# A decoder layer whose instruction order is planned by a list scheduler: new durations and ranks, q split before it is stored, gates kept as sums, small loads issued second

## The chip, the core and the metric

The kernel runs on one core of one Trainium2 chip. The core has five engines, each with an instruction queue of its own that is worked off in order: TensorE (PE, matmuls, with its weight loads shown apart as PEld), VectorE (DVE), ScalarE (ACT), GpSimd (POOL) and SyncE (SP, which here only issues DMA transfers). DMAs are also issued from the queues of ACT and POOL. The metric is the device time of one execution in microseconds; the median of several executions is compared.

## The reference

One layer (DEPTH = 1) on 1024 tokens of 1024 channels, in float32:

```python
h = rms_norm(x, g_mix_norm[l])
z = h @ w_in[l]
q, kc, vc, ks_, vs_, kw_, vw_, gl, hc, cg, bg = jnp.split(z, offs, axis=-1)
q = rms_norm(q.reshape(B, T, N_ATTN_HEADS, HEAD_DIM), g_q[l])
k_cmp = rms_norm(compress(kc...), g_k[l, 0])
v_cmp = compress(vc...)
k_slc = rms_norm(ks_.reshape(kv_shape), g_k[l, 1])
k_win = rms_norm(kw_.reshape(kv_shape), g_k[l, 2])
gates = jax.nn.sigmoid(gl).reshape(B, T, N_ATTN_HEADS, N_BRANCH)
attn_out = nsa_attention(q, k_cmp, v_cmp, k_slc, vs_, k_win, vw_, gates)
conv_out = short_conv_mixer(hc, cg, bg, conv_w[l])
mixed = jnp.concatenate([rms_norm(attn_out, ...), rms_norm(conv_out, ...)], axis=-1)
x = x + mixed @ w_o[l]
h = rms_norm(x, g_ffn_norm[l])
x = x + jnp.square(jax.nn.relu(h @ w_up[l])) @ w_down[l]
```

There are 8 query heads of 64 channels in 2 groups that share keys and values. Each head has three softmax branches with a distance penalty: over 63 compressed blocks, over selected blocks (with 1024 tokens all 16 blocks are chosen), and over a window of 512 tokens. Each branch's output is multiplied by its gate, sigmoid(gl) = 1 / (1 + exp(-gl)), and the three are added. `compress` is a small MLP with a tanh-approximated GELU over blocks of 32 tokens. The feed-forward part is 1024 to 4096 to 1024 with a squared ReLU.

## The kernel before

**Numbers and tiles.** Tokens are worked in eight blocks of 128 (`tb`). Each float32 factor of a matmul is split in a high part, rounded to the matmul's input type, and a low part, the rest; a product is three matmuls, high by high, high by low and low by high (`mm3`). A split is one ACT copy for the high part and one subtraction on DVE or POOL for the low one (`split_psum`, `w_piece`, `split`).

**Stages, in the order of the source.**
1. The token blocks are normalised and transposed (`norm_in`); five small loads fill the tile `rows` (norm gains, convolution weights, position terms), which PE transposes into `cols`; the weight splits scale by columns of `cols`.
2. The input projection by tokens (`z_tokens`): keys and values (stored to `kv_d` or split), then the window part with the gates, then q. Between its matmuls the steps of the compression MLP run (`compress_steps`: tiles `ch`, `araw`, `ah`, `al`, `hp`, `hx`, `hT`, `cps`).
3. The rest of the projection by channels (`z_chan`, tile `zc`) and the convolution.
4. The convolution's half of the output projection (`wc`), key transposes, and attention: per block of queries and group, `queries` loads and transposes q (`qx`, `tpq`, `Qg`, `Qz`), `scores` makes scores, row minima and exponentials, and `weigh` transposes the probabilities, multiplies by the values (`ot`, `ops`, `ot_s`, `osb`) and weighs with `rr`; `finish` adds attention's half of the output projection.
5. The up projection in 16 pairs (`pair`), as products of sums of quadrants (a seven-product scheme; operands B11, T2, ... and sums S1 to S4), whose results are stored in `u_d`; then the down projection in 8 rounds, which loads them again (`ur`, split as `uu`), splits the weight sums (`we`) and adds each result to `y`.

**Who sets the order.** Nothing of this runs in source order. Every operation is first recorded as a node of a `Plan`, with the nodes that it has to wait for; `cost` gives each its duration by engine, operation and columns; `schedule` then simulates the engines and orders the nodes, and `issue` emits them in that order. So the order inside each engine's queue is fixed beforehand; on the chip an instruction that waits holds everything behind it. All recorded operations carry one line number, L261, in the profile; they are told apart by their tiles. In `schedule` a node's rank (`prio`) is the longest path from it to the end, along its successors and the reuse of tile buffers; an engine that is free takes the ready node of highest rank. Before, up to four matmuls in a row on the same output tile are one node:

```python
GROUP = 4
```

An engine is busy for `busy`, and the result counts as there after `late`. All DMAs share one modelled line of 0.36 MB per us plus 1.75 us. Engines don't disturb each other in the model, only that DVE's two-input operations on 256 columns or more outside PSUM count 1.45 times; a power on POOL counts 0.5 us whatever its size.

**q before.** In the q loop of `trunk_layer`, a block's result is copied out of PSUM by ACT (`z`, two buffers), squared and reduced; POOL makes the reciprocal root by a power (`rsqrt`, with `rs_t` and `qri`); then eight multiplications on DVE, one for each head, write the normalised row twice, side by side, into `qn` (one buffer), and ACT issues the store to `q_d`. Later `queries` loads both copies, transposes them, ACT rounds both to the high part (`Qg`), and DVE subtracts in the half of partitions that shall hold the low part.

**Gates before.** `gates` holds 1 / (1 + exp(-gl)) for all tokens; `scores` takes the reciprocal of the three sums of exponentials (`sm`) and multiplies by the gates, one small DVE operation for each branch, into `rr`.

Of the kernel before, what the change touches and what calls it, by code (L numbers as in the profile page):

```python
# [18 lines left out]
P = 128  # L19
# [4 lines left out]
H = 8  # L24
# [109 lines left out]
class Node:  # L134
    def __init__(self, k, engine):
        self.k, self.engine, self.do, self.preds, self.succ = k, engine, [], set(), []
        self.busy = self.late = self.bytes = 0.0
        self.base, self.bases = None, []
# [11 lines left out]
class Plan:  # L150
# [82 lines left out]
    def op(self, name, engine, method, a, kw):  # L233
        views = [("" if i else "out", v) for i, v in enumerate(a)] + list(kw.items())
        views = [(k, v) for k, v in views if isinstance(v, View)]
        preds, touched = set(), []
        for k, v in views:
# [5 lines left out]
            for n, ow, o0, o1, om in v.base.seen:  # L243
                if (w or ow) and r0 < o1 and o0 < r1 and m & om:
                    preds.add(n.k)
        out = views[0][1] if views else None
        last = self.last_pe if name == "PE" else None
# [7 lines left out]
        node.preds |= preds  # L255
        if name == "PE":
# [12 lines left out]
        busy, late, size = self.cost(name, method, a, kw, views)  # L269
        node.late = node.busy + late  # L270
        node.busy += busy
        node.bytes += size
# [4 lines left out]
    GROUP = 4  # L277

    def cost(self, name, method, a, kw, views):
        n = max([v.cols() for _, v in views], default=1)  # L280
        psum = any(v.base.pool.psum for k, v in views if k not in ("out", "accum_out"))
        if method == "dma_start":
            nb = 4 * max(int(np.prod(v.shadow.shape)) for _, v in views)
            return (.75 if name == "POOL" else .33), 0.0, nb
        if name == "PE":
# [6 lines left out]
            return c, c + .17, 0  # L292
        if name == "ACT":
            c = .06 + n * .00093 if n >= 600 else max(.085 + n * .00079 if n > 100 else .17 + n * .0008, .17)
            acc = kw.get("accum_out") is not None
            return c + .1 * acc, c + (.1 if acc else .11), 0
        if name == "DVE":
            if method == "tensor_tensor_reduce":
                return .135 + n * .00125, .19 + n * .0013, 0
            if method == "tensor_tensor":  # L300
                c = (.06 + n * .00106) * (1.45 if not psum and n >= 256 else 1.0)
            elif method == "scalar_tensor_tensor":
                c = .06 + n * (.00112 if n > 600 else .00122)
            elif method == "tensor_scalar":
                c = .06 + n * .00085
            else:
                c = .06 + n * .00106
            return max(c, .08), c + .08, 0
        if method == "tensor_tensor":
            if kw.get("op") == ALU.pow:  # L310
                return .5, .56, 0
            c = .18 + n * .00215
            return c, c + .03, 0
        c = .15 + n * .0009 if method == "tensor_copy" else .12 + n * .0008 if method == "memset" else .2 + n * .002
# [3 lines left out]
    def schedule(self, weight=lambda n: 0.0, rings=True):  # L318
        nodes = self.nodes
        slots, held, left_of = {}, {}, {}  # L320
        for b in self.bases:
            slots[id(b.ring)] = [0.0] * b.ring[0]
            held[id(b.ring)] = []
            left_of[b] = [len(b.nodes), 0.0]
# [27 lines left out]
        for n in nodes:  # L352
            n.prio += weight(n)
# [4 lines left out]
        line, order, end = 0.0, [], 0.0  # L358
# [9 lines left out]
        while True:  # L368
            while stack:
                n = stack.pop()  # L370
                if n.engine is None:
                    if n.base is not None:
# [4 lines left out]
                        n.ready = max(n.ready, heapq.heappop(slots[ring]))  # L377
# [20 lines left out]
            n = nodes[heapq.heappop(ready[e])[1]]  # L398
            n.start = t
            free[e] = t + n.busy  # L400
            done = t + n.late
            if n.bytes:
                line = max(t + .4, line) + n.bytes / .36e6
                done = line + 1.75
            end = max(end, done)
            order.append(n)
            for b in n.bases:
                rest = left_of[b]
                rest[0] -= 1
                rest[1] = max(rest[1], done)  # L410
                if not rest[0]:
                    heapq.heappush(slots[id(b.ring)], rest[1])
                    stack.extend(held[id(b.ring)])
                    held[id(b.ring)] = []
            if n.bytes:
                settle(n, done)
            else:
                for s in n.succ:
                    s.left -= 1
                    s.ready = max(s.ready, t + n.busy if s.engine == n.engine else done + .05 * (s.engine is not None))  # L420
                    if not s.left:
                        stack.append(s)
# [15 lines left out]
def trunk_layer(ctx, tc, x, g_mix_norm, w_in, g_q, g_k, pe_cmp, w_cmp1, b_cmp1, w_cmp2, b_cmp2,  # L438
# [50 lines left out]
    gates = cst.tile([P, NT, 3 * H], F32, name="gates")  # L489
# [961 lines left out]
```

## Time and profile before

| | us |
|---|---|
| median of 3 runs | 1324.02 |
| lowest, highest | 1319.44, 1326.87 |
| the profiled execution | 1318.85 |
| its span, first to last instruction | 1317.1 |

The mean granted clock of TensorE in that execution was 0.991. How to read the rows that follow: an instruction row has its start, its duration, the engine, what it writes and reads, and, in brackets, how long the engine stood idle before it and what released it. A matmul's duration holds its passage through the array, so matmuls overlap; the rate is read from their starts. PE's busy time is the union of such stretches, so that a busy PE can still run slowly. ACTq and SPq mark DMA issues from the queues of ACT and SP. A duration from issue to landing is that of the whole transfer.

### The profile page before, as it was taken

The numbers are of one execution on the slowest core, as the hardware profiler recorded it, in microseconds if no ns is written. First come the engines' busy times: TensorE is split into PE (matmuls) and PEld (weight loads), VectorE is DVE, ScalarE is ACT, GpSimd is POOL, SyncE is SP. The second block draws the span as 40 slices with busy tenths as digits, with TensorE's granted clock in tenths as the row PEclk, the third lists the DMA queues.
The fourth block names the chain that finished last, engine by engine and source line by source line (L and its number), as shares of the span: only waits on it lengthen the run. The fifth ranks groups of instructions, "written<-read, shape, count | busy, mean of one in ns | idle before, by whom it ended". The sixth has DMA issues, their size and how long they took to land. (4 is left out here: it accounts for less than half of the span.)

```text
span 1317.1 us, 18392 instructions
## 1 busy us (share of the span) xinstructions
PE 1248.7 (95%) x6170; PEld 1031.2 (78%) x6170; DVE 909.9 (69%) x1869; ACT 674.1 (51%) x1498; POOL 672.9 (51%) x583
## 2 busy tenths in 40 slices
PE   6999899999889999999899999999999899999998
PEld 5897688888678888888777877777777687777787
DVE  6466864434698899998874655555657777887875
ACT  6343542211588988887956454445333343434441
POOL 2243311221133333112766877777879977788761
PEclk9999899999999999999899999999999999999999
DMA  6253431212310000000414435345339445443423
GB/s 223 77 137 112 127 90 51 73 38 80 112 65 33 33 33 33 25 15 4 128 64 168 135 137 168 123 149 168 137 134 395 142 160 168 152 130 122 149 64 128
DMA packets 91575, 147.66 MB, mean 112 GB/s; under 512 B 10901, under 2 KB 45801, under 8 KB 91481
## 3 DMA queue, kind: packets, MB, share of 16 engines
q1 hardware_dynamic: 87256, 134.51, 31.1%
q10 hardware_dynamic: 3456, 9.44, 1.9%
q0 software_dynamic: 768, 2.56, 0.7%
q8 instruction: 48, 0.79, 0.2%
q14 instruction: 47, 0.38, 0.1%
HBM read 102.43 MB, written 44.04 MB: 111 GB/s over the span
## 5 line engine op out<-in xcount | busy, mean ns | idle before, releaser
L261 PE MATMUL X<-we,uu 128*128 128x512 f32 x768 | 186.4, 393 | 13.3 <-DVE y L261 7.3
L261 PEld LDWEIGHTS X<-we,uu 128*128 128x128 f32 x768 | 144.0, 189 | 49.1 <-issue 7.0
L261 PE MATMUL Z<-we,uu 128*128 128x512 f32 x576 | 139.0, 392 | 2.7 <-DVE y L261 2.7
L261 PEld LDWEIGHTS Z<-we,uu 128*128 128x128 f32 x576 | 109.1, 190 | 25.9 <-ACT uu L261 3.1
L261 POOL TENSOR_TENSOR d<-d 128x512 f32<-128x512 f32 x64 | 96.8, 1523 | 21.7 <-DVE d L261 20.6
L261 ACT ACTIVATE we<-wd 128x512 fp32r<-128x512 f32 x64 | 40.5, 632 | 124.6 <-PE X L261 83.6
L261 DVE TENSOR_TENSOR y<-X,y 128x512 f32<-128x512 f32 x128 | 79.4, 681 | 33.8 <-PE X L261 33.7
L261 DVE TENSOR_TENSOR pl<-tp,ph 128x512 fp32r<-128x512 f32 (+1 forms) x148 | 95.2, 655 | 9.1 <-ACT ph L261 8.6
L261 ACT ACTIVATE pt<-pt,nm 128x640 f32<-128x640 f32 (+7 forms) x128 | 93.8, 735 | 11.5 <-DVE nm L261 11.2
L261 POOL TENSOR_TENSOR uu<-ur,uu 128x512 fp32r<-128x512 f32 x56 | 80.0, 1432 | 32.7 <-ACT uu L261 32.7
L261 ACT ACTIVATE ph<-tp 128x512 fp32r<-128x512 f32 (+1 forms) x148 | 82.5, 573 | 20.1 <-PE tp L261 18.2
L261 PE MATMUL tp<-ident,pt 128*128 128x128 f32 x528 | 88.7, 275 | 3.4 <-ACT pt L261 1.7
L261 DVE SCALAR_TENSOR_TENSOR w_lo<-w_raw,cols,w_hi 128x128 fp32r<-128x128 f32 (+3 forms) x128 | 56.0, 491 | 43.3 <-ACT w_hi L261 43.2
L261 PEld LDWEIGHTS tp<-ident,pt 128*128 128x128 f32 x528 | 65.5, 140 | 21.2 <-ACT pt L261 4.3
L261 ACT ACTIVATE w_hi<-w_raw,cols 128x128 fp32r<-128x128 f32 (+3 forms) x128 | 53.1, 486 | 54.5 <-PE zc L261 27.0
L261 DVE TENSOR_TENSOR we<-s,we 128x512 fp32r<-128x512 f32 x42 | 41.6, 990 | 56.4 <-ACT we L261 51.9
L261 DVE TENSOR_TENSOR uu<-ur,uu 128x512 fp32r<-128x512 f32 x56 | 66.7, 1195 | 17.8 <-ACT uu L261 17.8
L261 ACT ACTIVATE wu<-wu,cols 128x256 f32<-128x256 f32 x128 | 55.8, 509 | 37.2 <-DMA wu<-in_w_up_dram 37.2
L261 DVE TENSOR_TENSOR we<-wu,we 128x512 fp32r<-128x512 f32 x38 | 50.5, 1341 | 34.1 <-ACT we L261 34.1
L261 PE MATMUL zc<-hTl,w_hi 128*128 128x512 f32 x192 | 71.8, 389 | 0.0
L261 DVE TENSOR_TENSOR y<-Z,y 128x512 f32<-128x512 f32 x96 | 59.5, 682 | 17.6 <-PE Z L261 17.6
L261 POOL TENSOR_TENSOR osb<-osb,ot_s 128x256 f32<-128x256 f32 x64 | 48.4, 756 | 45.2 <-DVE ot_s L261 39.1
(1262 smaller groups left out, 3562.6 us busy)
## 6 DMA issues: line engine op xcount, KB each, us to landing
u_d<-d SPq DMA_DIRECT2D x112, 256.0 KB, 2.1
ur<-u_d SPq DMA_DIRECT2D x112, 256.0 KB, 3.0
wu<-in_w_up_dram SPq DMA_DIRECT2D x16, 1024.0 KB, 6.0
wd<-in_w_down_dram SPq DMA_DIRECT2D x16, 1024.0 KB, 6.8
w_raw<-in_w_in_dram SPq DMA_DIRECT2D x20, 512.0 KB, 3.7
xt<-in_x_dram SPq DMA_DIRECT2D x10, 512.0 KB, 5.6
w_raw<-in_w_cmp_dram SPq DMA_DIRECT2D x8, 512.0 KB, 4.0
q_d<-qn ACTq DMA_DIRECT2D x8, 512.0 KB, 2.6
```

What stands on the lines that cost most here:

```text
L261: node.do.append(lambda: getattr(engine, method)(*[real(x) for x in a], **{k: real(x) for k, x in kw.items()}))
```

## The change

It has five parts.

1. **The planner's nodes and rank.** Every matmul is a node of its own (`GROUP = 1`), and a PE node depends on the PE node before it on the same output tile. To the rank comes `-.03` us for each node number, so that, of two equal paths, what stands earlier in the source goes first, and `plan.plus` by hand for a few loads.
2. **Durations.** `cost` has new formulas for nearly every operation, among them the power on POOL, 0.4 + 0.15 us a column.
3. **One path for DVE and POOL, waits and queues.** Operations of DVE without a PSUM input and of POOL, of 64 columns or more, take turns on one modelled path (`port`); an instruction that has to wait for several others at once is held 0.09 us for each beyond the first; no more than eight DMAs issued from SP are under way at a time; and an operation that reads what its own engine wrote waits for the result.
4. **q and gates.** The eight multiplications write the normalised row once, in place, in `z`; ACT copies it by groups into the half of `qn` that shall hold the high part, POOL subtracts into the other, and SP issues the store. In `queries` the subtraction on DVE is gone. `gates` holds 1 + exp(-gl), laid out as `scores` needs it; the sum and the gate's sum are multiplied in the operation that also guards the sum, and one reciprocal follows.
5. **Small loads.** The first token block is loaded first, then the five loads of `rows`, then the rest.

```diff
-    GROUP = 4
+    plus = 0.0
+    GROUP = 1
...
+        if name == "PE":
+            preds.update([n.k for n in out.base.nodes if n.engine == "PE"][-1:])
...
+        near = not psum
         if name == "ACT":
-            c = .06 + n * .00093 if n >= 600 else max(.085 + n * .00079 if n > 100 else .17 + n * .0008, .17)
+            c = (.1 if near else .05) + n * .000834
+            if any(isinstance(kw.get(k), View) for k in ("scale", "bias")):
+                c += .09
...
-            if method == "tensor_tensor":
-                c = (.06 + n * .00106) * (1.45 if not psum and n >= 256 else 1.0)
-            elif method == "scalar_tensor_tensor":
-                c = .06 + n * (.00112 if n > 600 else .00122)
+            if method == "scalar_tensor_tensor":
+                c = .1 + n * .0011 if n >= 200 else .11 + n * .0012
...
+                c = .064 + n * .00104
+            self.port = near and n >= 64
+            return c, c + .08, 0
+        self.port = n >= 64
         if method == "tensor_tensor":
             if kw.get("op") == ALU.pow:
-                return .5, .56, 0
-            c = .18 + n * .00215
+                return .4 + .15 * n, .45 + .15 * n, 0
+            c = .15 + n * .00213
...
-    def schedule(self, weight=lambda n: 0.0, rings=True):
+    def schedule(self, weight=lambda n: -.03 * n.k, rings=True):
...
-            n.prio += weight(n)
+            n.prio += weight(n) + n.plus
...
+            if n.bytes and e != "POOL":
+                if len(landed) >= 8 and landed[-8] > t + 1e-6:
+                    heapq.heappush(wait[e], (landed[-8], n.k))
+                    continue
             n.start = t
-            free[e] = t + n.busy
-            done = t + n.late
...
+            hold = n.hold = .09 * max(0, len(new) - 1)
...
+            if n.port:
+                hold += max(0.0, port - t - hold)
+                port = t + hold + n.busy
+            free[e] = t + hold + n.busy
+            done = t + hold + n.late
...
+        plan.plus = 100.0
         nc.sync.dma_start(xts[0], x2d[0:P])
+        plan.plus = 50.0
         rows = xp.tile([68, P], F32, name="rows", bufs=1)
...
+        plan.plus = 0.0
...
-            nc.vector.tensor_scalar(e, e, 1.0, None, op0=ALU.add)
-            nc.vector.reciprocal(gates[:, tb], e)
+            for g in range(G):
+                eg = e[:, g * 12:(g + 1) * 12].rearrange("p (i j b) -> p b j i", i=2, b=3)
+                nc.vector.tensor_scalar(gates[:, tb, g].rearrange("p b (j i) -> p b j i", j=2), eg, 1.0, None,
+                                        op0=ALU.add)
...
-            qn = zt.tile([P, H, 2, HD], F32, name="qn", bufs=1)
+            qn = zt.tile([P, H, 2, HD], F32R, name="qn", bufs=1)
             for h in range(H):
-                nc.vector.scalar_tensor_tensor(qn[:, h], dup(z[:, h * HD:(h + 1) * HD]), ri[:, h:h + 1],
-                                               dup(gq_bc), op0=ALU.mult, op1=ALU.mult)
-            nc.scalar.dma_start(q_d[tb * P:(tb + 1) * P], qn.rearrange("p h a d -> p (h a d)"))
+                c = slice(h * HD, (h + 1) * HD)
+                nc.vector.scalar_tensor_tensor(z[:, c], z[:, c], ri[:, h:h + 1], gq_bc, op0=ALU.mult, op1=ALU.mult)
+            for g in range(G):
+                zg = z[:, g * 256:(g + 1) * 256].rearrange("p (r d) -> p r d", r=R)
+                qg = qn[:, g * R:(g + 1) * R]
+                copy_act(qg[:, :, g], zg)
+                tt(nc.gpsimd, qg[:, :, 1 - g], zg, qg[:, :, g].bitcast(F32), ALU.subtract)
+            nc.sync.dma_start(q_d[tb * P:(tb + 1) * P], qn.rearrange("p h a d -> p (h a d)").bitcast(F32))
...
-            nc.vector.tensor_scalar(rr, sm, 1e-30, None, op0=ALU.max)
+            nc.vector.scalar_tensor_tensor(rr, sm, 1e-30, gates[:, tb, g], op0=ALU.max, op1=ALU.mult)
             nc.vector.reciprocal(rr, rr)
-            gt = gates[:, tb, g * 12:(g + 1) * 12].rearrange("p (i j b) -> p b j i", i=2, b=3)
-            rv = rr.rearrange("p b (j i) -> p b j i", j=2)
-            for b in range(3):
-                tt(nc.vector, rv[:, b], rv[:, b], gt[:, b], ALU.mult)
...
-                lo = half[1 - g]
-                nc.gpsimd.memset(Qz[lo].bitcast(F32), 0.0)
+                nc.gpsimd.memset(Qz[half[1 - g]].bitcast(F32), 0.0)
                 nc.gpsimd.tensor_copy(Qz[half[g]], Qg[half[g]])
-                tt(nc.vector, Qg[lo], tp[lo], Qg[lo].bitcast(F32), ALU.subtract)
```

More of the change, by code (lines that the diff above doesn't have):

```diff
@@ L321, in schedule @@
         for b in self.bases:
-            slots[id(b.ring)] = [0.0] * b.ring[0]
+            slots[id(b.ring)] = [(0.0, i, {}) for i in range(b.ring[0])]
             held[id(b.ring)] = []
-            left_of[b] = [len(b.nodes), 0.0]
+            left_of[b] = [len(b.nodes), 0.0, {}]
+            b.last = {x[0].k for x in b.seen if not x[1]} or {x[0].k for x in b.seen}
         for n in nodes:
@@ L357, in schedule @@
         ready = {e: [] for e in names}
-        line, order, end = 0.0, [], 0.0
+        seen = {e: {} for e in names}
+        soft, landed, line, port, order, end = 0, [], 0.0, 0.0, [], 0.0
         stack = [n for n in reversed(nodes) if not n.preds]
@@ L488, in trunk_layer @@
     cols = cst.tile([P, 68], F32, name="cols")
-    gates = cst.tile([P, NT, 3 * H], F32, name="gates")
+    gates = cst.tile([P, NT, G, 3, R], F32, name="gates")
     rconv = cst.tile([P, NT], F32, name="rconv")
```

72 lines of the change are left out of this document (52 added, 20 removed).

## The prediction

> **What bounds the kernel now.** I read the busy shares first, then TensorE's idle time stage by stage, then what ended each idle stretch.
>
> ```profile
> span 1317.1 us, 18392 instructions
> PE 1248.7 (95%) x6170; PEld 1031.2 (78%) x6170; DVE 909.9 (69%) x1869; ACT 674.1 (51%) x1498; POOL 672.9 (51%) x583
> ```
>
> TensorE is busy 95% of the span. The change neither adds nor removes a matmul or a transpose, so the most that any order can win is the idle remainder, 1317.1 - 1248.7 = 68.4 us, plus what lies inside busy time at a slow clock. Where those 68 us lie is shown by the busy time by stage (stretch, its length, then busy us and instructions of PE, weight loads, DVE, ACT and POOL, granted clock, DMA share, GB/s); I cut the stretches where the stage of the kernel changes.
>
> ```profile
> 0.00:15.00 15.00, 4.16 (x18) 3.57 (x18) 4.21 (x14) 7.64 (x13) 4.75 (x21) 1.00 0.85 259
> 15.00:111.00 96.00, 95.20 (x549) 84.31 (x549) 62.34 (x147) 50.26 (x115) 32.26 (x47) 1.00 0.44 128
> 111.00:172.00 61.00, 50.93 (x252) 42.38 (x251) 44.09 (x137) 24.03 (x59) 17.28 (x12) 0.94 0.35 114
> 172.00:340.00 168.00, 167.26 (x763) 138.41 (x763) 71.96 (x142) 37.91 (x94) 29.09 (x29) 1.00 0.21 64
> 340.00:480.00 140.00, 129.90 (x784) 105.89 (x782) 123.67 (x437) 119.93 (x351) 45.52 (x69) 0.99 0.18 61
> 480.00:640.00 160.00, 158.82 (x1000) 135.98 (x1000) 144.70 (x445) 134.08 (x304) 38.58 (x57) 1.00 0.11 38
> 640.00:690.00 50.00, 44.75 (x228) 35.92 (x228) 39.83 (x52) 33.08 (x67) 39.57 (x30) 0.93 0.17 56
> 690.00:920.00 230.00, 224.39 (x978) 182.18 (x977) 124.83 (x129) 115.77 (x238) 170.16 (x114) 1.00 0.45 150
> 920.00:1080.00 160.00, 145.58 (x621) 117.55 (x620) 109.86 (x126) 63.48 (x113) 130.28 (x90) 0.98 0.55 198
> 1080.00:1280.00 200.00, 195.32 (x850) 158.51 (x849) 162.42 (x215) 82.47 (x143) 158.58 (x111) 1.00 0.41 131
> 1280.00:1317.10 37.10, 32.37 (x143) 26.47 (x141) 21.97 (x33) 5.46 (x10) 6.83 (x5) 1.00 0.31 114
> ```
>
> PE's idle is length minus the first number: 10.8 at the start, 0.8, 10.1 in the q projection (111 to 172), 0.7 in the channel projection, 10.1 in the first half of attention, 1.2 in the second, 5.3 where attention ends, 5.6 in the up projection, 14.4 where up hands over to down, 4.7 in the down projection, 4.7 at the end. So five places hold 51 of the 68 us. The list of PE's waits (what waited, for whom: us in total, times, longest) names the largest single ones:
>
> ```profile
> PE cps L261 <- issue: 7.9, 2, 7.6
> PE tp L261 <- DVE rs_t L261: 7.3, 1, 7.3
> PE X L261 <- DVE y L261: 7.3, 6, 3.2
> PE tp L261 <- DMA rows<-in_g_out_dram: 3.5, 1, 3.5
> PE Z L261 <- DVE y L261: 2.7, 1, 2.7
> ```
>
> **The q projection: rank and durations, and the moved write.** The 7.6 us hole is best seen in the order of time, all engines:
>
> ```profile
> 126.87 0.33 ACTq L261 DMA_DIRECT2D q_d<-qn  x1
> 127.24 0.60 ACT L261 ACTIVATE z<-zp 128x512 f32<-128x512 f32 x1 [5.47 <-DVE qn L261]
> 129.26 0.17 DVE L261 TENSOR_SCALAR rs_t<-qss 128x8 f32<-128x8 f32 x1
> 129.51 1.64 POOL L261 TENSOR_TENSOR qri<-rs_t,mhalf 128x8 f32<-128x8 f32 x1 [5.09 <-DVE rs_t L261]
> 131.18 0.17 DVE L261 TENSOR_TENSOR qri<-qri,qscale 128x8 f32<-128x8 f32 x1 [1.75 <-POOL qri L261]
> 131.86 3.19 DVE L261 SCALAR_TENSOR_TENSOR qn<-z,qri,gq_bc 128x128 f32<-128x128 f32 x8
> 135.57 0.41 DVE L261 COPY hT<-tp 128x256 f32<-128x256 f32 x1
> 136.08 1.09 PE L261 MATMUL cps<-w,hT 128*128 128x64 f32 x4 [7.60 <-issue]
> ```
>
> ACT stands 5.47 us at the write q_d<-qn, which it issues itself and which waits for DVE's eight multiplications; only then can it copy the next projection result out of PSUM. So each token block goes through one serial loop of about 5.47 + 0.60 + 0.6 for the square = 6.7 us, while its 24 matmuls need less:
>
> ```profile
> 1052.73 3.63 PE Z L261 x16
> ```
>
> That row of the chain of waits gives 3.63 / 16 = 0.227 us for a 512-column matmul, hence 24 x 0.227 = 5.4 us a block. PE therefore runs out of free PSUM banks. Second, DVE stands 1.75 us at the multiplication qri, since POOL's power of 8 columns took 1.64 us where the old planner counts 0.5; the copy hT, on which cps waits, stands behind it at 135.57.
>
> The change moves the write from ACT's queue to SP's, counts 0.4 + 0.15 x 8 = 1.6 us for the power, halves the columns of the eight DVE multiplications (128 to 64), and adds per block two ACT copies and two POOL subtractions of 256 columns. A copy of 256 columns isn't in the trace; it lies between nothing and the 0.60 us of the 512-column copy above, and I take 0.6 for safety. The subtraction has the shape of a row of the attention stage:
>
> ```profile
> L261 POOL TENSOR_TENSOR osb<-ot_s x16: 721/732/740, 371.5 to 638.7; 128x256 f32<-128x256 f32 x16
> ```
>
> So POOL gains 16 x 0.73 = 11.7 us on the 17.3 of 61 that it is busy there. Two new loops must stay under 5.4 us a block. The single buffer qn: two copies 1.2, the last subtraction 0.73, and the write, which lands 2.6 us after its issue:
>
> ```profile
> q_d<-qn ACTq DMA_DIRECT2D x8, 512.0 KB, 2.6
> ```
>
> Sum 4.5. The two buffers z: the life of one from its copy at 127.24 to the end of the multiplications at 131.86 + 3.19 = 135.05 is 7.8; the new work adds 1.9; half of 9.7 is 4.9. Both fit, the second barely, so PE becomes the bound. Of the 10.1 idle I take 8 as won (the tanh chain of the compression stays); bounds 2 (another engine of the loop holds) and 11, since the hole also leaves slow matmuls behind it:
>
> ```profile
> 136.93 0.77 PE L261 MATMUL zp<-w_hi,hTh 128*128 128x512 f32 x1
> ...
> 139.21 0.50 PE L261 MATMUL zp<-w_lo,hTh 128*128 128x512 f32 x1
> ```
>
> Five matmuls start between these two, (139.21 - 136.93) / 5 = 0.46 us each, twice 0.227: 1.1 us lost. The Trainium skill (TensorE: Matmul & The Clock Gate, section What's actually happening) says that an idle window of some 3.4 us halves the clock and a busy one of that length restores it; the doubled 0.46 us agrees, and by the page's full window the hole would have cost up to 1.7 us more instead of 1.1, and the sum below would be 0.6 us larger.
>
> On SP the eight writes now wait in turn for POOL's subtraction; queued behind each are the weight loads (compression, then channel projection), and PE's zc matmuls wait for those. The cover is the double-buffered weights: one piece of the channel projection is 48 x 0.227 = 10.9 us of PE work, and that stage idles 0.7 us in 168. I cost it at nothing; without the cover, one late piece is up to 2.6 us.
>
> **Small loads second.**
>
> ```profile
> 4.39 0.32 SPq L261 DMA_DIRECT2D rows<-in_g_out_dram  x1
> ...
> 12.81 0.37 PE L261 MATMUL tp<-ident,rows 68*128 68x68 f32 x1 [3.55 <-DMA rows<-in_g_out_dram]
> ...
> 13.36 0.68 DVE L261 TENSOR_TENSOR hTl<-tp,hTh 128x512 fp32r<-128x512 f32 x1
> ...
> 14.54 0.78 PE L261 MATMUL zp<-w_hi,hTh 128*128 128x512 f32 x1
> ```
>
> The last of five small loads is issued at 4.39, behind two token tiles and a weight piece, and arrives 8.4 us later. PE waits 3.5 us, DVE's hTl stands behind the copy of those rows, and the first projection matmul starts at 14.54. Issued right behind the first token tile, the rows should be there when PE starts at 7.3. Bounds: 12.81 - 7.29 = 5.5 won, or nothing, if the weight piece, issued five slots later, is then what is late. I take 3.
>
> **Attention: less on DVE.**
>
> ```profile
> L261 DVE TENSOR_TENSOR Qg<-tpq,Qg x16: 677/688/696, 340.1 to 554.9; 64x512 fp32r<-64x512 f32 x16
> ...
> L261 DVE TENSOR_TENSOR rr<-rr,gates x48: 147/157/643, 370.5 to 628.0; 128x4 f32<-128x4 f32 x48
> ```
>
> Both groups go: 16 x 0.688 + 48 x 0.157 = 18.5 us of DVE. The max keeps its place as one operation with the gate. Half the head groups, 9.3 us, fall in 340 to 480, where DVE is busy 123.7 of 140 and PE idles 10.1. But ACT is busy 119.9 there and loses nothing. Bounds 0 and 9.3; I take 4, nearer to the ACT bound. In 480 to 640 PE idles only 1.2: nothing. Eight gate reciprocals fewer, ahead of 111, lie beside a PE busy 95.2 of 96: nothing.
>
> **Single matmuls as nodes, new durations, rank falling with age.** These reorder everything. Interleaving banks matmul by matmul costs PE nothing: the X and Z runs of the chain go at the same 0.227. Past 640 PE idles 5.3 + 5.6 + 14.4 + 4.7 = 30 us outside the last tail. A planner that knows better what DVE and POOL cost may close part, or open new holes. Bounds: half closed, 15 won; or 28 lost (rival below). I take 4 won.
>
> **Sum:** 8 + 3 + 4 + 4 = 19 us. The profiled execution took 1318.85 (span 1317.1 and 1.75 around it), 5.2 under the median of the three runs; 1318.85 - 19 = 1300 for such an execution, 1324.02 - 19 = **1305** as a median.
>
> **Rivals.**
>
> *The order wins more.* q 10, start 4, attention 8, and 12 of the 30 us behind 640: 34 us, 1290. For it: the old costs miss the trace by factors (0.5 against 1.64). Against it: the handover's 14.4 us stand where POOL is busy 130 of 160, which no order shortens.
>
> *The loop only changes its engine.* z is still freed too late (4.9 against 5.4 leaves 10%), so q wins 2, the start 3, attention nothing because ACT holds it, the rest loses 1: 4 us, 1320. Differences below 0.5%, 6.6 us, can't be told from none here.
>
> *Slower: the path of DVE and POOL in up and down.* This path is nearly the bound of the down projection already:
>
> ```profile
> L261 DVE TENSOR_TENSOR uu<-ur,uu x56: 678/1330/1779, 989.1 to 1286.9; 128x512 fp32r<-128x512 f32 x56
> L261 POOL TENSOR_TENSOR uu<-ur,uu x56: 1272/1294/1777, 990.8 to 1286.4; 128x512 fp32r<-128x512 f32 x56
> ```
>
> DVE's subtraction takes 0.68 alone and up to 1.78: it waits out most of a POOL operation. In one round of the down loop (168 matmuls, 38.1 us of PE) POOL has 22 such operations and DVE 14, 22 x 1.294 + 14 x 0.678 = 38.0 us, if they exclude each other. A plan that leaves the path unused for over about 1.5 us a round makes it the bound. A round in which one bank then waits as the Z row above (2.7 us) costs 2.7; over the 590 us from 690 to 1280, some 15 rounds of 39.5, that is 40, against 15 won elsewhere: 1324 + 25 = 1349. It decides from (15 + 6.6) / 15 = 1.4 us a round. For it: every order in this region is new, and the rank by age pulls against the longest path. Against it: the old plan, which knows nothing of the path, loses under 1 us a round in 1080 to 1280, and the new one counts it. The Trainium skill (SBUF — State Buffer, section Who interferes with whom) says that a DVE instruction with two SBUF inputs and a GpSimd one that reads SBUF exclude each other for the whole instruction; the 1.78 us agree. By it this rival stands as priced; were the path shared in time instead, its price would fall toward nothing and I would give it half its chance.
>
> **How the numbers follow.** Forecast 0.50, more 0.16, loop only changes its engine 0.13, slower 0.21. The forecast's own bounds, from the terms (8 down to 2, attention 0, rest 0) and (11, 5, 9, 8), run from 1324 - 5 to 1324 - 33; nearly all of it is faster by 6.6. The range 1287 to 1336 leaves out a little of the second case and about half of the slower one. Faster 0.65, same 0.14, slower 0.21.
>
> **What would show it.** PE idle in the q stage under 4 us and no ACT wait on qn; the first zp matmul near 11.5; PE idle in the first attention half near 6; rounds of the down loop still at 39.5. I am wrong if PE's idle from 690 to 1280 grows past 40 us, if the q stage shows a wait on z or on SP's loads, or if the first zp matmul still starts past 14.

## The result, and the profile after

| | before | after |
|---|---|---|
| median, us | 1323.31 (4 runs, 1319.44 to 1326.87) | 1286.34 (4 runs, 1286.31 to 1287.37) |
| ratio | | 0.9723, 95% interval 0.9695 to 0.9751 |
| the profiled execution; its span | 1318.85; 1317.1 | 1286.31; 1284.2 |

The kernel became 37 us faster, nearly twice the 19 us that were forecast, and its time lies 0.7 us below the low end of the range. The page of the changed kernel begins:

```profile
span 1284.2 us, 18498 instructions
...
PE 1241.2 (97%) x6170; PEld 1026.9 (80%) x6170; DVE 898.5 (70%) x1805; ACT 691.3 (54%) x1514; POOL 681.3 (53%) x599
```

PE has the same 6170 matmuls. Its idle time is 1284.2 - 1241.2 = 43.0 us instead of 68.4, and its busy time is 7.5 us less. So of the 32.9 us of span, 25.4 were visible waits and 7.5 lay inside busy time. About half of the 7.5 is the clock. The kernel before has five stretches at half the granted clock (from 132.6, 388.6, 644.6, 989.3 and 1026.9, 3.4 or 6.8 us each), the changed kernel two (289.7 and 965.6) and its last 1.2 us; PE is busy for 17.9 us of them before and 10.2 after, which costs 8.9 and 5.1 us, 3.8 less. That the other 3.7 us are hidden waits is likely and not measured: a 512-column matmul shows as 0.39 us but the next can start 0.227 us after it, so that a wait of up to 0.16 us looks busy.

Busy time by stage, same columns as before:

```profile
111.00:172.00 61.00, 61.00 (x304) 50.80 (x303) 47.17 (x155) 32.96 (x85) 31.27 (x29) 1.00 0.43 137
172.00:340.00 168.00, 165.50 (x747) 136.25 (x746) 76.48 (x153) 40.49 (x101) 32.25 (x31) 0.98 0.19 60
340.00:480.00 140.00, 132.24 (x812) 109.41 (x811) 114.00 (x398) 121.89 (x349) 46.99 (x71) 1.00 0.17 57
480.00:640.00 160.00, 155.73 (x990) 132.64 (x989) 143.65 (x411) 137.56 (x312) 44.66 (x59) 1.00 0.12 42
640.00:690.00 50.00, 48.40 (x245) 38.90 (x245) 35.98 (x48) 29.18 (x57) 37.80 (x30) 1.00 0.20 67
690.00:920.00 230.00, 227.74 (x1000) 186.51 (x999) 135.64 (x133) 123.61 (x243) 173.59 (x120) 1.00 0.47 156
920.00:1080.00 160.00, 155.06 (x671) 125.94 (x669) 126.12 (x148) 70.40 (x118) 139.34 (x97) 0.99 0.60 212
1080.00:1280.00 200.00, 197.80 (x861) 160.28 (x860) 155.69 (x213) 79.05 (x128) 138.46 (x99) 1.00 0.38 122
```

The hole of the q stage is gone (61.00 of 61). From 640 to 1280 PE idles 1.6 + 2.3 + 4.9 + 2.2 = 11 us, where it idled 30. In the first half of attention (340 to 480) it idles 7.8 us, where 6 were forecast. But since the stages now begin earlier, equal stretches don't hold equal work. I therefore cut both traces at the same work: the last zc matmul (the projections are done), the last wc matmul (the convolution's half of the output projection), and the last ot matmul (attention is done). PE's order of time, before and after:

```profile
291.74 0.39 PE L261 MATMUL zc<-hTh,w_lo 128*128 128x512 f32 x1
...
639.76 0.28 PE L261 MATMUL ot<-pl,vco 128*128 128x256 f32 x1
```

```profile
282.81 0.39 PE L267 MATMUL zc<-hTh,w_lo 128*128 128x512 f32 x1
...
631.53 0.28 PE L267 MATMUL ot<-pl,vco 128*128 128x256 f32 x1
```

The projections end 8.9 us earlier, the stretch from there to the end of attention is 348.7 us against 348.0, and what follows attention takes 652.7 us against 677.3. So 24.6 us of the 32.9 were won behind attention, in the up and down projections, where the change touches no operation at all. The stretch from the last ot matmul to the end, before and after:

```profile
639.76:1317.10 677.34, 642.66 (x2815) 520.71 (x2813) 459.14 (x553) 300.51 (x568) 505.43 (x349) 0.99 0.43 147
```

```profile
631.53:1284.20 652.67, 635.11 (x2806) 516.24 (x2804) 462.22 (x549) 310.70 (x565) 497.62 (x349) 1.00 0.45 153
```

PE's idle time there fell from 34.7 to 17.6 us and its busy time by 7.5, about 3.9 of these through fewer stretches at half the clock. A round of the down loop, 168 matmuls, took 39.5 us from the third round on, and 47.8 and 41.9 in the first two; now it takes 38.6 to 39.0, and 42.6 and 38.9. The forecast had the rounds still at 39.5.

The same cut for the main runs below, each from its one profiled execution, in us; "first zp" is the start of the first projection matmul:

| kernel | first zp | to last zc | to last wc | to last ot | to the end | median, ratio to before |
|---|---|---|---|---|---|---|
| before | 14.5 | 291.7 | 51.2 | 296.8 | 677.3 | 1323.31 |
| after | 15.5 | 282.8 | 60.3 | 288.4 | 652.7 | 1286.34, 0.9723 |
| a1: new planner, old operations | 13.2 | 280.9 | 60.2 | 297.5 | 654.2 | 1295.91, 0.9771 |
| a2: old planner, new operations | 14.9 | 296.4 | 50.6 | 286.6 | 681.5 | 1315.99, 0.9918 |
| d1: before, one duration | 14.8 | 284.8 | 50.3 | 295.8 | 679.9 | 1315.69, 0.9929 |
| a4: after without the path | 16.0 | 288.3 | 57.1 | 290.5 | 671.4 | 1309.04, 0.9867 |
| b1: after without the rank by age | 17.2 | 284.2 | 57.4 | 292.2 | 661.5 | 1297.32, 0.9784 |
| b2: after with old durations | 15.3 | 290.9 | 57.5 | 296.2 | 658.3 | 1303.95, 0.9836 |
| c1: after, one old duration | 15.6 | 290.2 | 57.1 | 289.4 | 653.6 | 1291.96, 0.9737 |
| d6: after, two matmuls a node | 15.9 | 284.7 | 55.1 | 289.0 | 644.6 | 1275.11, 0.9617 |
| a3: after, four a node | 17.6 | 285.1 | 53.8 | 292.8 | 643.6 | 1276.62, 0.9624 |
| d7: after, twelve a node | 18.3 | 284.1 | 50.8 | 292.0 | 651.0 | 1277.72, 0.9639 |

Each ratio is to executions of the kernel before that were timed next to the run; their medians lie between 1323.31 us (beside the changed kernel) and 1326.85. Two kernels timed at different occasions can therefore be compared only to some 3 us.

The changed kernel's PE waits (what waited, for whom: us in total, times, longest) show what is left:

```profile
PE tp L267 <- DMA rows<-in_pe_cmp_dram: 5.8, 1, 5.8
PE tp L267 <- DVE rs_t L267: 4.6, 1, 4.6
PE X L267 <- ACT uu L267: 4.0, 2, 2.7
...
PE s__2825 L267 <- DVE sqs L267: 2.5, 1, 2.5
PE Z L267 <- ACT d L267: 2.3, 4, 1.4
...
PE X L267 <- DVE y L267: 1.6, 4, 0.5
...
PE Z L267 <- DVE y L267: 0.6, 2, 0.4
```

The waits of X and Z for DVE's y, 10.0 us before, are 2.2.

### The profile page after: what moved, and what is told of

The parts are those of the page before. It is cut to its first block, busy times and chain, and to the rows that moved or that the text cites. A ratio compares the mean times of both kernels' runs of the same rounds, so it can differ in the third digit from the quotient of the medians.

```text
span 1284.2 us, 18498 instructions
## 1 busy us (share of the span) xinstructions
PE 1241.2 (97%) x6170; PEld 1026.9 (80%) x6170; DVE 898.5 (70%) x1805; ACT 691.3 (54%) x1514; POOL 681.3 (53%) x599
## 3 DMA queue, kind: packets, MB, share of 16 engines
q10 hardware_dynamic: 2304, 5.24, 1.1%
## 4 chain that ended last, share of the span: by engine, by line
PE 84%; DVE 5%; ACT 5%; DMA 4%; issue 2%; POOL 0%; SPq 0%; DVEq 0%; ACTq 0%; POOLq 0%
PE X L267 24%; PE Z L267 15%; PE zc L267 10%; PE zp L267 8%; PE tp L267 6%; PE ot L267 4%; PE wc L267 3%; PE wa L267 3%; PE W L267 3%; DMA wu<-in_w_up_dram 1%; PE ops L267 1%; DVE y L267 1%; PE hp L267 1%; ACT pt L267 1%; ACT wu L267 1%
## 5 line engine op out<-in xcount | busy, mean ns | idle before, releaser
L267 PE MATMUL X<-we,uu 128*128 128x512 f32 x768 | 193.2, 393 | 5.7 <-ACT uu L267 4.0
L267 PE MATMUL Z<-we,uu 128*128 128x512 f32 x576 | 147.4, 391 | 0.6 <-DVE y L267 0.6
L267 ACT ACTIVATE uu<-ur 128x512 fp32r<-128x512 f32 x112 | 69.1, 631 | 123.3 <-PE X L267 62.2
L267 PE MATMUL tp<-ident,pt 128*128 128x128 f32 x528 | 100.8, 273 | 2.2 <-ACT pt L267 1.3
L267 DVE TENSOR_TENSOR y<-X,y 128x512 f32<-128x512 f32 x128 | 79.6, 680 | 15.9 <-PE X L267 15.3
L267 DVE SCALAR_TENSOR_TENSOR w_lo<-w_raw,cols,w_hi 128x128 fp32r<-128x128 f32 (+3 forms) x128 | 61.6, 525 | 23.6 <-ACT w_hi L267 23.4
L267 ACT ACTIVATE we<-wu 128x512 fp32r<-128x512 f32 x57 | 35.7, 632 | 58.6 <-PE X L267 45.8
L267 DVE SCALAR_TENSOR_TENSOR d<-d 128x512 f32<-128x512 f32 x48 | 64.9, 1353 | 0.9
## 6 DMA issues: line engine op xcount, KB each, us to landing
u_d<-d SPq DMA_DIRECT2D x112, 256.0 KB, 4.1
ur<-u_d SPq DMA_DIRECT2D x112, 256.0 KB, 2.7
```

The source lines that it names most:

```text
L267: node.do.append(lambda: getattr(engine, method)(*[real(x) for x in a], **{k: real(x) for k, x in kw.items()}))
```

## The experiments

### Planner or operations

a1 puts the old operations under the new planner, a2 the new operations under the old one; the cut goes through the file at `trunk_layer`. So a1 is the changed file with everything from `trunk_layer` on as before, without the ranks by hand for the loads; a2 is the file before with the changed operations. In a2 the lines `plan.plus = ...` stand too, but the old `schedule` doesn't read them.

> The new planner (nodes, rank, durations, path, waits) on the old operations: q, gates and the order of the small loads as before. Theory A, the order made most of the gain, since 27 us of the 33 us of span came after 640 us, where no operation was changed: 1293 to 1303. Rival B, the removed DVE work and the moved write made it and the planner only fits them in: 1310 to 1318, with the hole of 7 us in the q stage still there.

> The old planner on the new operations (q split before the store, store on SP, gates as sums). Theory A: only the q stage gains, 8 us, and attention little: 1311 to 1318, PE idle behind 690 us as before (25 us). Rival B: 1290 to 1303.

a1 took 1295.91 us (0.9771, 0.9754 to 0.9788), a2 1315.99 (0.9918, 0.9903 to 0.9933). Both times lie where theory A had them: the order alone wins 30 us, the operations alone 11. For a2 that is partly luck, since theory A laid its gain on the q stage and had little for attention. The table says where the gains are. Behind attention a1 wins 23 us and a2 nothing. In attention itself, last wc to last ot, it is the other way round: the operations win 9 to 10 us under either planner (296.8 to 286.6, and 297.5 to 288.4), the planner nothing. And a2's projections take 4.7 us longer than before, with the hole of the q stage still there, though the store was moved to SP; theory A had forecast 8 us won there.

```profile
PE cps L261 <- ACT qn L261: 8.7, 1, 8.7
```

ACT's own order of time in a2 shows why:

```profile
120.47 0.58 ACT L261 ACTIVATE z<-zp 128x512 f32<-128x512 f32 x1
...
125.55 0.42 ACT L261 ACTIVATE qn<-z 128x256 fp32r<-128x256 f32 x1 [3.83 <-DVE z L261]
126.28 0.42 ACT L261 ACTIVATE qn<-z 128x256 fp32r<-128x256 f32 x1 [0.32 <-DVE z L261]
126.61 0.58 ACT L261 ACTIVATE z<-zp 128x512 f32<-128x512 f32 x1
```

ACT no longer stands at the store, but at the copies that now precede it, and the next z is again copied out of PSUM only after them: one block takes 126.61 - 120.47 = 6.14 us, still above PE's 5.4.

### The hole of the q stage

d1 changes one line of the kernel before; c1 changes the same line back in the changed kernel; b4 returns the store to ACT there.

```diff
# d1, in cost of the kernel before; c1 the reverse in the changed kernel
             if kw.get("op") == ALU.pow:
-                return .5, .56, 0
+                return .4 + .15 * n, .45 + .15 * n, 0
# b4, in the changed kernel
-            nc.sync.dma_start(q_d[tb * P:(tb + 1) * P], qn...)
+            nc.scalar.dma_start(q_d[tb * P:(tb + 1) * P], qn...)
```

> The kernel before with one line of its planner changed: a power on POOL counts 0.4 us plus 0.15 for each column, where it counted 0.5. If that duration made the q stage's hole, the hole of 7.6 us shrinks below 3 with the write still on ACT and q still stored twice, and the last zc matmul comes 6 to 9 us earlier: 1315 to 1320. If it was the write or the serial loop, as the prediction had it, the hole stays: 1322 to 1330.

> The changed kernel whose planner counts 0.5 us again for a power on POOL, all else new. If the hole of the q stage came from that one duration (1.64 us traced), it is back: a PE wait of 5 us or more between 110 and 170, 1291 to 1295. If it came from the order of the whole stage, no such wait, and 1284 to 1289.

> The changed kernel with the store of q issued from ACT again. If the move to SP is worth what the prediction laid on it, ACT stands at each store and the q stage loses 5 us or more: 1291 to 1296. If the planner places the store where q is ready, nothing: 1284 to 1289.

d1 took 1315.69 us (0.9929, 0.9899 to 0.996): one number in the plan is worth about 9 us, with q stored twice and from ACT as before. Its ACT shows how:

```profile
118.97 0.33 ACTq L261 DMA_DIRECT2D q_d<-qn  x1
121.76 0.60 ACT L261 ACTIVATE z<-zp 128x512 f32<-128x512 f32 x1 [4.18 <-PE zp L261]
122.39 0.63 ACT L261 ACTIVATE qsq<-z 128x512 f32<-128x512 f32 x1
124.21 0.33 ACTq L261 DMA_DIRECT2D q_d<-qn  x1
```

The next block's z is now copied ahead of the store of this one, and ACT waits for PE instead of PE for ACT: a block takes 124.21 - 118.97 = 5.24 us. The likely way: counting 0.5 us for the power of 8 columns (1.64 us traced), the old plan held that the store would be ready before the next z, and put it first; no run shows the plan's own times. c1 took 1291.96 us (0.9737, 0.9711 to 0.9764). Its interval overlaps that of the changed kernel, but its trace is plain: the projections end at 290.2 instead of 282.8, and PE idles 5.8 us in the q stage, where the changed kernel idles none.

```profile
111.00:172.00 61.00, 55.22 (x271) 45.37 (x270) 43.80 (x148) 31.95 (x81) 33.96 (x28) 0.97 0.36 114
```

The longest single wait there is 3.8 us, not the 5 or more that were expected. b4 took 1288.41 us (0.9721, 0.9693 to 0.9748), no different from the changed kernel. Here the store's queue is worth nothing that shows once the order is right.

### The path of DVE and POOL, durations, rank by age

```diff
# a4
-        node.port = self.port
+        node.port = False
# b1
-    def schedule(self, weight=lambda n: -.03 * n.k, rings=True):
+    def schedule(self, weight=lambda n: 0.0, rings=True):
# b2: the durations of the kernel before, with the new path, waits and rank
```

> The changed kernel whose planner lets DVE and POOL run beside each other without the shared path, all else new. Theory D: the path is what the order needs in up and down, where POOL and DVE together fill it: 1294 to 1305, with rounds of the down loop back at 39.5 us. Rival C: the in-order engines wait for the path on the chip anyway, so the plan hardly matters: 1284 to 1290, rounds near 38.5.

> The changed kernel with the rank as the longest path alone (no 0.03 us off for each node number). Measured so far: the new planner loses about 10 us between the last zc and the last ot matmul and wins 23 after it. Theory E, the rank by age makes that loss, since it holds back the key transposes and scores that attention needs first: that stage 5 to 10 us shorter, 1276 to 1283. Rival F, the rank by age is part of what wins behind attention: 1292 to 1302.

> The changed kernel with the old durations in its planner, the shared path, the waits and the rank as new. Theory D2, path and durations go together, since the path is nearly full and wrong lengths fill it wrongly: 1295 to 1312, and the q stage's hole of 7 us is back. Rival G, the rules alone carry the gain: 1284 to 1291.

a4 took 1309.04 us (0.9867, 0.9852 to 0.9883), 23 us more than the changed kernel by the times and 19 by the ratios, and more than either theory had: 18.7 of them lie behind attention. The rounds of the down loop are 40.0 us long; theory D had 39.5. Its waits of PE from 690 to 1300:

```profile
PE Z L267 <- DVE y L267: 9.0, 7, 3.2
PE Z L267 <- ACT d L267: 7.9, 5, 1.7
```

In each of the last six rounds Z waits 0.97 us for y, and DVE's y stands behind a subtraction of DVE that takes 1.77 us beside POOL's, where one alone takes 0.68:

```profile
1135.10 0.68 DVE L267 TENSOR_TENSOR we<-wd,we 128x512 fp32r<-128x512 f32 x1
1135.70 1.77 DVE L267 TENSOR_TENSOR uu<-ur,uu 128x512 fp32r<-128x512 f32 x1
1137.40 2.47 DVE L267 TENSOR_TENSOR y<-Z,y 128x512 f32<-128x512 f32 x4
```

ACT's d, in the up projection, stands behind the scaling of the next weights, for which ACT waited on a load:

```profile
788.66 1.70 ACT L267 ACTIVATE wu<-wu,cols 128x256 f32<-128x256 f32 x4 [3.32 <-DMA wu<-in_w_up_dram]
790.27 0.61 ACT L267 ACTIVATE we<-s 128x512 fp32r<-128x512 f32 x1
790.79 0.57 ACT L267 ACTIVATE d<-Z 128x512 f32<-128x512 f32 x1
```

Why that load is late in this plan stays open. b1 took 1297.32 us (0.9784, 0.9756 to 0.9812): rival F held, the rank by age wins 9 us behind attention; theory E fell, the stretch from the last zc to the last ot stayed at 349.6. b2 took 1303.95 us (0.9836, 0.9808 to 0.9864), a time as theory D2 had it, though the hole of 7 us is back only in part (from 111 to 180 PE idles 5.9 us, in waits of at most 2.4): 8 us of its loss lie in the projections, as much as c1's single duration explains, 5 from there to the end of attention, and 5.6 behind it.

### Matmuls in a node

```diff
-    GROUP = 1
+    GROUP = 4      # a3; 2 in d6, 12 in d7
```

> The changed kernel with up to four matmuls in one node again, all else new. Theory C, single matmuls as nodes let PE go on with another bank while one waits, and that is most of what was won behind 640 us: 1298 to 1310. Rival D, it is the new durations and the shared path, and a node of four costs under 1 us a round: 1285 to 1291.

> The changed kernel with up to two matmuls in a node. With one it takes 1286, with four 1277. If fine nodes cost time steadily (each matmul of a chain adds its own 0.17 us of lateness to the rank, and PE turns between banks before either is done), two lie between: 1279 to 1284. If four was a lucky order, anything from 1275 to 1295, outside that band as likely as in it.

> The changed kernel with up to twelve matmuls in a node (a whole product of the up projection). By the steady cost of fine nodes: at or under the 1277 of four, 1270 to 1278. Rival: long nodes hold PE at a matmul whose operands are late and block other banks, 1280 to 1300.

All three beat the changed kernel: 1276.62 us with four (0.9624, 0.9609 to 0.9639), 1275.11 with two (0.9617, 0.9595 to 0.9639), 1277.72 with twelve (0.9639, 0.9605 to 0.9672). Theory C had the sign wrong, and rival D missed too: single nodes cost 11 us against nodes of two by the times and 14 by the ratios, 8.1 of them behind attention. A steady cost of fine nodes, by which two should have lain between, fell too; it is the step from one to two. The chain of waits of the changed kernel shows a sight that goes with it:

```profile
1104.90 0.45 PE Z L267 x2
1105.35 0.23 PE X L267
1105.58 0.45 PE Z L267 x2
1106.03 0.45 PE X L267 x2
1106.49 0.45 PE Z L267 x2
```

PE goes to and fro between two banks every matmul or two, so both are done late, and DVE gets two sums to add at once instead of one after the other. But d6 shows runs of the same kind, in the same stretch, and takes less time; that this turning costs the 11 us is argued, not shown.

### What the planner loses in front of attention

a1 and the changed kernel need 60 us from the last zc to the last wc, the other kernels with single nodes 57 to 59, the kernels with the old planner 50 to 51. Stretches of the changed kernel and of a2 for that piece:

```profile
283.00:343.00 60.00, 57.51 (x272) 46.88 (x271) 25.74 (x60) 12.96 (x33) 9.96 (x14) 0.94 0.24 84
```

```profile
296.00:347.00 51.00, 50.58 (x250) 42.22 (x249) 20.60 (x35) 6.36 (x14) 8.80 (x13) 1.00 0.28 93
```

PE idles 2.5 us (it waits for DVE's sums of squares sqs, below), loses 3.4 us to the clock after that (half the clock for 6.8 us), and does 22 instructions of attention more, an estimated 3 us at the 0.13 us of a 256-column matmul or a transpose here: 9 us together, of which the last three are only work done earlier. Of the kernels with single nodes, a4 and c1 have no such stretch in this piece and need 57.1.

```profile
289.69 1.86 PE L267 MATMUL s__2825<-ones,sqs 128*128 128x1 f32 x8 [2.50 <-DVE sqs L267]
```

Four more runs each leave out a rule of the planner that could be behind it, on nodes of two matmuls: no hold for several waits (e1), no limit of eight DMAs (e2), no wait within an engine (e3), and none of the three (e4).

```diff
# e1
-            hold = n.hold = .09 * max(0, len(new) - 1)
+            hold = n.hold = 0.0
# e2
-            if n.bytes and e != "POOL":
+            if False:
                 if len(landed) >= 8 and landed[-8] > t + 1e-6:
# e3
-                own = s.engine == e and not n.bytes and (e == "PE" or n.k not in s.raw)
+                own = s.engine == e and not n.bytes
```

> The version with two matmuls in a node (1275, stage from the last zc to the last ot matmul 344 us), whose planner adds no 0.09 us for each further wait. If the extra holds make the planner think that the many small operations of attention are slower than they are, and lose there, that stage is 4 to 10 us shorter: 1265 to 1272. If not: 1273 to 1282.

> The same version, whose planner lets any number of DMAs be under way. If the limit of eight places the loads of q and x late (PE waits for qx in the changed kernel), attention is 2 to 6 us shorter: 1269 to 1274. If the limit is right on the chip, the plan without it issues loads that then hold SP, and up and down lose: 1277 to 1290.

> The same version, whose planner lets an operation start right after another of its own engine whose result it reads. If that wait spreads the short chains of attention (row minimum, max, reciprocal) and so loses there, the stage is 3 to 8 us shorter: 1267 to 1273. If not: 1273 to 1285.

> The same version without all three (no hold, no limit, no wait within an engine): path, durations, rank by age and nodes of two are left. If the loss of attention comes from these three together, its stage is near the 337 us that the old planner reaches with the new operations, and the time 1266 to 1271. If it comes from the path or the rank, the stage stays at 344 or more and the time at 1275 or more.

They took 1275.72, 1277.17, 1278.43 and 1275.30 us (0.9644, 0.9643, 0.9657 and 0.9630, each within 0.003), against 1275.11 (0.9617): no difference here is clear of the noise, neither way, and the piece in front of attention stayed at 55 us. With single nodes and no loss of clock it is 57.1, with nodes of two 55.1, with four 53.8, with twelve 50.8, as before. So the nodes are part of it, the clock is another, and no part of the three rules shows.

### The small loads

```diff
# b3: the second block ahead of the small loads
         nc.sync.dma_start(xts[0], x2d[0:P])
+        nc.sync.dma_start(xts[1], x2d[P:2 * P])
         plan.plus = 50.0
...
-        nc.sync.dma_start(xts[1], x2d[P:2 * P])
# f1 (and f2, with GROUP = 2)
-        plan.plus = 100.0
+        plan.plus = 0.0
...
-        plan.plus = 50.0
+        plan.plus = 0.0
```

> The changed kernel with the second token block loaded right after the first, ahead of the five small loads. In the changed kernel ACT stands 5.5 us at the square of that block, and the copies hTh of the first block stand behind it. If that wait set the first projection matmul at 15.5, it comes at 11 to 13 and the time is 1282 to 1284. If the start is bound by the weight pieces, the first matmul stays past 14.5 and the time at 1285 to 1288.

> The changed kernel without the ranks by hand for the first block and the small loads, so that the planner places them. If small loads second is a gain of its own, as the prediction had it (3 us), the first projection matmul comes later than 15.5 and the time is 1288 to 1291. If it only changed which load is late, the first projection matmul comes at 13 to 15 and the time is 1283 to 1287.

> Two matmuls in a node and no ranks by hand, everything else as in the changed kernel; meant as a version that beats both. If the two edits add up: 1272 to 1276. If the start doesn't matter: as with nodes of two alone, 1274 to 1277.

In the changed kernel the small loads are there when the forecast had them, and another load is late, on ACT:

```profile
5.83 0.35 PE L267 MATMUL tp<-ident,rows 68*128 68x68 f32 x1 [5.83 <-DMA rows<-in_pe_cmp_dram]
...
13.92 1.97 PE L267 MATMUL tp<-ident,xt 128*128 128x128 f32 x8 [4.57 <-DVE rs_t L267]
15.54 0.78 PE L267 MATMUL zp<-w_hi,hTh 128*128 128x512 f32 x1
```

```profile
11.11 1.06 ACT L267 ACTIVATE junk<-xt 128x1024 bf16<-128x1024 f32 x1 [5.47 <-DMA xt<-in_x_dram]
...
13.41 1.07 ACT L267 ACTIVATE hTh<-tp 128x512 fp32r<-128x512 f32 x2
```

ACT stands 5.47 us at the second token block, and the copies hTh of the first block, ready since 9, stand behind it. b3 repairs that wait, but then the small loads come at 10.4, and ACT stands 4.3 us at the third block instead; its first zp is at 14.6 and its time 1286.33 us (0.9698, 0.9674 to 0.9722), as without. f1, where the planner places the loads itself, has the first zp at 13.1 and 1285.04 us (0.9707, 0.9686 to 0.9727), and f2 1274.48 us (0.9624, 0.9603 to 0.9645). So the ranks by hand win nothing; the interval of f1 doesn't tell whether they lose the 1 to 2 us that the first matmul suggests. f2 and d6 have the lowest times of the study, about 11 us under the changed kernel; they can't be told apart, nor from a3, e1 and e4.

## Why the prediction was right and wrong

**The bound and the q hole's size: right.** PE was the bound and stayed it. The projections end 8.9 us earlier; 8 were forecast for q, and the waits there vanished. The slow matmuls behind the hole were put at 1.1 us; the stretch at half the clock (132.6 to 139.4) holds 3.3 us of busy PE, so 1.7 were lost.

**The q hole's cause: wrong.** The prediction laid it on the store that ACT issues and on a serial loop of 6.7 us, and counted on the moved store and the halved multiplications. a2 has both and keeps the hole (8.7 us), d1 has neither and loses it, b4 moves the store back without harm. The loop of 6.7 us was no property of the operations; the row of 5.47 us of waiting on ACT was an order, in which the store stood ahead of the next z. The prediction did name the power's wrong duration, but as a second matter of 1.75 us. So the 8 us came out right in size by luck.

**Small loads, 3 us: wrong.** The first zp came 1.0 us later, not 3 us earlier. The prediction named a late weight piece as the bound that could take the gain; it was the second token block, on the queue of another engine.

**Attention, 4 us: mis-sized and then hidden.** The changed operations, with 18.5 us of DVE work removed, are worth 9 to 10 us there (a2 against before, after against a1), about its upper bound of 9.3. The assumed limit, ACT busy for 119.9 of 140, did not hold. That both engines feed the same short chains, and that taking work off either shortens these, would explain it and is argued, not shown. In the result the gain doesn't show, since the planner gives 9 us back in front of attention.

**The order behind attention, 4 us: this step failed.** It was a small part of the visible 30 us of idle, "half closed, 15 won" its upper bound. Measured: 24.6 us, and 23.1 with the old operations. In equal stretches about 19 of the 30 visible us closed, in the handover 14.4 to 4.9; cut at the same work, 17.1 us of the 24.6 were visible waits and the rest lay in busy time, half of it the clock. The sentence that no order shortens the handover because POOL is busy 130 of 160 there fell: POOL is now busy 139 of 160 in the same stretch, and PE idles a third. A busy sum says what an engine can't fall below, not that the work comes in the right order. With that sentence the prediction had kept the rival of a larger gain (34 us, 1290) at a chance of 0.16. That rival comes near in total, but by luck: of its terms only q, 10 us, fits. It had 12 us behind 640, half of what came, 4 at the start, where 1 was lost, and 8 in attention, where nothing was left. What the gain rests on is shown by leaving parts of the planner out: without the path 18.7 us behind attention are lost, without the rank by age 8.8, with the old durations 5.6; together 33.1, against 24.6 won and 8.1 that single nodes take back. Such parts need not add up, and that they nearly do may be chance.

**The path of DVE and POOL: right mechanism, wrong side.** The reckoning that it is filled to 38.0 of 39.5 us in a round of the down loop was made for the slower rival. a4 shows the other face of it: where a resource is that full, a plan that knows of it wins, 19 to 23 us here. The Trainium skill (SBUF — State Buffer, section Who interferes with whom) has the shared ports of the two engines as an exclusive lock, for which a DVE instruction with two SBUF inputs and a GpSimd one that reads SBUF contend; the gain from planning so agrees with it, as do DVE's subtractions uu, from 0.68 to 1.78 us before and to 1.80 after.

**Single matmuls as nodes, "costs PE nothing": wrong.** PE's rate stayed at 0.227 us, but the order made of single matmuls costs 11 us against nodes of two; why is not shown.

## What to carry to other kernels

When the order is planned, an engine's wait in the trace is first of all a statement on the plan: look for the duration or the shared resource that the plan has wrong before blaming the operation at which the engine stands; one corrected number removed the hole here that a rebuilt q stage had left in place. As the upper bound of a better plan take all of the visible idle time of the stages that it reorders and some of the busy time, not half of the idle time; here 24.6 us came where 34.7 were visible. When one late load is moved up, name the next load, on every queue, that the same engine waits for.

## What was not expected of the hardware

A short wait can cost PE more in clock than the wait itself. In the changed kernel PE stands 2.50 us for sqs, up to 289.69, and the stretch that follows has half the granted clock (third number from the end):

```profile
289.70:296.50 6.80, 6.80 (x22) 5.69 (x23) 0.85 (x2) 0.60 (x1) 2.06 (x2) 0.50 0.24 77
```

Half of 6.8 us, 3.4 us of full-speed work, is lost there, beside the wait. In the kernel before a wait of 1.71 us is followed by 3.4 us at half the clock:

```profile
388.07 0.50 PE L261 MATMUL wa<-w_hi,mh 128*128 128x512 f32 x1 [1.71 <-DVE ml L261]
```

```profile
388.60:392.00 3.40, 3.40 (x10) 2.56 (x10) 2.84 (x14) 0.94 (x4) 0.56 (x1) 0.50 0.42 157
```

But a wait of 3.18 us there, which ends at 1048.82, is followed by the full clock. So length alone doesn't decide. The slow stretches of that kernel begin on a grid: 132.6, 388.6 and 644.6 are 256.0 us apart, 75 times the 3.413 us that the shortest of them lasts. The Trainium skill (TensorE: Matmul & The Clock Gate, section What's actually happening) speaks of free-running windows of some 3.4 us, of which 6.8 would be two; grid and lengths agree with that, though the waits of 1.71 and 2.50 us were shorter than one window.

How much of the lost clock is lost time differs. The kernel before took 1320.29 us at a mean clock of 0.991 and 1329.30 at 0.983, but the changed kernel took 1286.34 us both at 0.996 and at 0.998.
